# A hybrid encoder layer on one core: the diagonal's mask moves from GpSimd into the logits' PSUM bank

## The chip, the cores and the metric

The kernel runs on one core of a Trainium2 chip. The core has a matrix engine (TensorE, PE in the profile; its weight loads are PEld), a vector engine (VectorE, DVE), an activation engine (ScalarE, ACT), a general engine (GpSimd, POOL) and SyncE (SP), which only issues DMAs. The engines run at the same time. Each takes its own instructions strictly in order and waits on semaphores. TensorE writes to PSUM, which has eight banks of 128 x 512 float32; GpSimd works on SBUF alone in this kernel, VectorE and ScalarE on both.

The metric is the device time of one execution in microseconds; less is better.

## The reference

One layer on 2048 tokens of width 1024: a norm, a projection, three mixers side by side (two short convolutions and a stick-breaking attention), an output projection, then a squared-ReLU MLP of width 4096 and a last norm. The change touches the attention, and one step of the norms. The attention, for each block of 128 queries:

```python
z = jnp.einsum("bhqd,bhkd->bhqk", qb, kb).astype(jnp.float32) * scale   # scale = 1/8
mask = s_idx < t_idx
log_beta = jax.nn.log_sigmoid(z)
log_1m = jnp.where(mask, log_beta - z, 0.0)
suffix = lax.cumsum(log_1m, axis=3, reverse=True) - log_1m
a = jnp.where(mask, jnp.exp(log_beta + suffix), 0.0)
out = jnp.einsum("bhqk,bhkd->bhqd", a, vb)
```

In products instead of logarithms: a = sigmoid(z) times the product of sigmoid(-z) over all later allowed keys. A key that the mask forbids must give sigmoid(z) = 0 and sigmoid(-z) = 1.

## The kernel before

All matrix products are split in two float32r halves, high and low, so that most products are three matmuls (`mm3`), and many tensors are split (`split`, lines 85 to 90): ScalarE copies the high half, VectorE or GpSimd subtracts it.

The work has two stages. The first makes the projections, the convolutions and, woven between them, the attention of the first 512 queries (i = 0) for the eight heads. The second runs four blocks of 512 tokens (`block`, line 818): output projection, then 32 units of the first MLP product (`ffn1`, tile ps_u) and eight groups of the second (`ffn2`, tile ps_y, added into `acc` by VectorE in line 944). Between the matmuls of the first three blocks lies the attention for i = 1, 2, 3: 24 groups (head, i) of 512 queries. `weave` (line 57) lets the attention advance in step with the main work. This gives the order in which the program is written; a planner then orders each engine's instructions by a model of their times, and each engine keeps that order on the chip.

A group goes through these steps:

- `a_load` (line 489): GpSimd issues the two DMAs of tile KQd, the group's own keys and queries. There is one buffer; it comes free after the last logits of the group before.
- `a_pass1` (line 539), first part: three diagonal steps n = 0, 1, 2, each on two blocks of 128 x 256. `a_z` (line 509) makes the logits z by matmuls into a bank with tag z (three banks in the second stage). `a_diag` (line 524) takes two sigmoids by ScalarE (`om` of -z, line 529, `t` of z, line 530) into SBUF and masks both by GpSimd's affine_select (line 534; fill 1 and 0). Then products: the left half of `om` into the right half of `t` (GpSimd, lines 558 and 566), and the halves of `om` into the running products `Rd` and `R` (VectorE, lines 559, 568, 573, 575); GpSimd multiplies the third `t` by `R` (line 574).
- `a_cross_a` (line 603): VectorE transposes `Rd` into `T` in 32 x 32 blocks, a scan (line 611) makes the products along the keys into tile `O`, small products (line 619) join the four parts, and line 625 writes the result back to `T`.
- for i > 0, 4i steps with all 128 x 512 logits of earlier keys (lines 585 to 600): ScalarE puts sigmoid(z) in SBUF and sigmoid(-z) back in z's own bank, GpSimd multiplies (line 595), VectorE goes on with the product `R` from the bank (line 597). Then `a_cross_a` again.
- `a_pass2` (line 629): VectorE transposes the result into PSUM (ps_q) and multiplies each `t` by it (lines 646, 653), the product is split by ScalarE and GpSimd (lines 88, 90, tiles Ahi, Alo), and TensorE multiplies it by the values into ps_o.

In `block`, after the first two units of `ffn1`, the mean square is spread over a bank with tag z (`spread`, line 130); ScalarE copies it to SBUF as `ms` (line 963), and VectorE multiplies the eight tiles `acc` by it (line 965).

`A0`, `om`, `R`, `O` and so on are tiles of pools with a fixed number of buffers; `self.ab` (line 1050 for the second stage) holds these numbers. The function `finish_` makes the last norm of a block; it too uses banks with tag z.

Of the kernel before, what the change touches and what calls it, by code (L numbers as in the profile page):

```python
# [7 lines left out]
F32 = mybir.dt.float32  # L8
F32R = mybir.dt.float32r
I32 = mybir.dt.int32  # L10
AF = mybir.ActivationFunctionType
ALU = mybir.AluOpType
# [3 lines left out]
P = 128  # L16
# [3 lines left out]
TB = 512  # L20
# [5 lines left out]
HP = 200  # L26
PRE = 4
LEFT = (0, 0, 0, 1, 0, 0, 0, 1)
RMS_EPS = 1e-6
LN_EPS = 1e-5  # L30

# [37 lines left out]
class Trunk:  # L69
# [126 lines left out]
    def attention_consts(self, ctx):  # L196
        nc = self.nc
        c = ctx.enter_context(self.tc.tile_pool(name="aconsts", bufs=1))
        self.d1 = c.tile([P, 16, 33], F32, name="d1")
        nc.vector.memset(self.d1, 0.0)  # L200
        nc.vector.memset(self.d1[:, :, 32:33], 1.0)


    def p_pools(self, ctx):
# [57 lines left out]
    def norm_sum(self, g):  # L262
        self.rv[g] = self.rsqrt(self.colsum([self.ss[g]], "o" if g else "q"), 1.0 / D, RMS_EPS)

# [256 lines left out]
        k = keys.rearrange("c (a p b) -> c a p b", a=2, b=J // 2)  # L521
        return [k[:, j % 2, :, j // 2] for j in range(J)]

    def a_diag(self, z, n):

        nc, pool, ab = self.nc, self.at, self.ab
        t = pool.tile([P, TB], F32, name="A0", tag="A0", bufs=ab["A0"])
        om = pool.tile([P, TB], F32, name="om", tag="om", bufs=ab["om"])
        nc.scalar.activation(om, z, AF.Sigmoid, scale=-0.125)
        nc.scalar.activation(t, z, AF.Sigmoid, scale=0.125)  # L530
        base, cm = ((-1, -2), (256 - 3, -4), (256 - 1, -4))[n]
        for x, fill in ((om, 1.0), (t, 0.0)):
            x = x.rearrange("p (h c) -> p h c", h=2)
            nc.gpsimd.affine_select(
                out=x, in_=x, pattern=[[1, 2], [1, 256]], compare_op=ALU.is_gt, fill=fill, base=base, channel_multiplier=cm
            )
        return t, om

    def a_pass1(self, g):
        nc, pool, i = self.nc, self.at, g["i"]  # L540
        ab = self.ab
        lo, hi2 = slice(0, 256), slice(256, 512)

        def new(name, bufs, shape=(P, TB), dt=F32):
            return pool.tile(list(shape), dt, name=name, tag=name, bufs=bufs)

        if i:
            g["Kl"] = pool.tile([P, self.kmax], F32R, name="Kl", tag="Kl", bufs=self.ab["Kl"])
            for rows, kq in self.kq_halves(g["h"]):
                to = g["Kl"][rows, : TB * i].rearrange("c (j q) -> c j q", j=2)  # L550
                self.load_r(to, kq[:, 0, :, : TB * i // 2])
        A0 = g["A0"] = []
        Rd = new("Rd", 1)

        k2 = [g["Kd"][:, 0:P], g["Kd"][:, 256 : 256 + P]]
        z = self.a_z(g, [(k2[1], lo, lo), (k2[0], lo, hi2)])
        t, om = self.a_diag(z, 0)
        nc.gpsimd.tensor_tensor(t[:, hi2], t[:, hi2], om[:, lo], op=ALU.mult)
        nc.vector.tensor_tensor(Rd[:, lo], om[:, lo], om[:, hi2], op=ALU.mult)
        A0.append(t)  # L560
        yield 1

        k4 = self.every(g["Kd"], 4)
        z = self.a_z(g, [(k4[3], hi2, lo), (k4[2], hi2, hi2)])
        t, om = self.a_diag(z, 1)
        nc.gpsimd.tensor_tensor(t[:, hi2], t[:, hi2], om[:, lo], op=ALU.mult)
        R = new("R", ab["R"])
        nc.vector.tensor_tensor(R[:, lo], om[:, lo], om[:, hi2], op=ALU.mult)
        A0.append(t)
        yield 1  # L570
        z = self.a_z(g, [(k4[1], hi2, lo), (k4[0], hi2, hi2)])
        t, om = self.a_diag(z, 2)
        nc.vector.tensor_tensor(R[:, hi2], om[:, lo], R[:, lo], op=ALU.mult)
        nc.gpsimd.tensor_tensor(t, t, R, op=ALU.mult)
        nc.vector.tensor_tensor(Rd[:, hi2], om[:, hi2], R[:, hi2], op=ALU.mult)
        A0.append(t)
        yield 1
        tot = self.a_cross_a(g, Rd, None)
        if not i:
            return  # L580
        J = 4 * i
        kl = self.every(g["Kl"][:, : TB * i], J)
        full = slice(0, TB)
        R = None
        for j in range(J - 1, -1, -1):
            z = self.a_z(g, [(kl[j], full, full)])
            t = new("A0", ab["A0"])
            if R is None:
                nc.scalar.activation(t, z, AF.Sigmoid, scale=0.125)
                R = new("R", 2)  # L590
                nc.scalar.activation(R, z, AF.Sigmoid, scale=-0.125)
            else:
                nc.scalar.activation(t, z, AF.Sigmoid, scale=0.125)  # L593
                nc.scalar.activation(z, z, AF.Sigmoid, scale=-0.125)  # L594
                nc.gpsimd.tensor_tensor(t, t, R, op=ALU.mult)  # L595
                Rn = new("R", 2)
                nc.vector.tensor_tensor(Rn, z, R, op=ALU.mult)  # L597
                R = Rn
            A0.append(t)
            yield 1  # L600
        self.a_cross_a(g, R, tot)

    def a_cross_a(self, g, R, seed):

        nc, pool = self.nc, self.at
        T = pool.tile([P, 16, 33], F32, name="T", tag="T1" if seed is None else "T2", bufs=1)
        nc.gpsimd.memset(T[:, :, 32:33], 0.0)
        nc.vector.transpose(T[:, :, 0:32], R)
        O = pool.tile([P, 16, 33], F32, name="O", tag="O", bufs=1)
        fl = lambda x: x.rearrange("p a b -> p (a b)")[:, ::-1]  # L610
        nc.vector.tensor_tensor_scan(fl(O), fl(T), fl(self.d1), 1.0, op0=ALU.mult, op1=ALU.add)
        C = self.tiny.tile([P, 16], F32, name="C", tag="C", bufs=3)
        if seed is None:
            nc.gpsimd.memset(C[96:128], 1.0)
        else:
            nc.vector.tensor_copy(C[96:128], seed)
        for a in (2, 1, 0):
            s, d = slice(32 * a + 32, 32 * a + 64), slice(32 * a, 32 * a + 32)
            nc.vector.tensor_tensor(C[d], C[s], O[s, :, 0], op=ALU.mult)
        tot = None  # L620
        if seed is None:
            tot = self.tiny.tile([32, 16], F32, name="tot", tag="tot", bufs=2)
            nc.vector.tensor_tensor(tot, C[0:32], O[0:32, :, 0], op=ALU.mult)
        qt = T[:, :, 0:32]
        nc.vector.tensor_tensor(qt, O[:, :, 1:33], C.unsqueeze(2).to_broadcast([P, 16, 32]), op=ALU.mult)
        g["qd" if seed is None else "ql"] = qt
        return tot

# [189 lines left out]
    def block(self, tb, before):  # L818
# [3 lines left out]
        nc, a, hp = self.nc, self.a, self.hp  # L822
# [34 lines left out]
        ss = hp.tile([P, TB], F32, name="ss", tag="ss", bufs=2)  # L857
# [35 lines left out]
        fh, fl = {}, {}  # L893
# [64 lines left out]
        mt = self.small("mt")  # L958
        nc.vector.tensor_scalar(mt, self.colsum([ss], "z"), 1.0 / D, RMS_EPS, op0=ALU.mult, op1=ALU.add)
        em = self.small("em")  # L960
        nc.vector.scalar_tensor_tensor(em, mt, RMS_EPS, mt, op0=ALU.mult, op1=ALU.mult)
        ms = hp.tile([P, TB], F32, name="ms", tag="ss", bufs=2)
        nc.scalar.activation(ms, self.spread(mt, "z"), AF.Copy)
        for d in range(DC):
            nc.vector.tensor_tensor(acc[d], acc[d], ms, op=ALU.mult)
        ss2 = hp.tile([P, TB], F32, name="ss2", tag="ss", bufs=2)
# [14 lines left out]
        else:  # L981
# [4 lines left out]
            with self.tc.high_priority(offset=HP):  # L986
                for n, _ in enumerate(ffn2(FC // G - 1, right, again=1)):
                    for _ in range(LEFT[n]):
                        next(fin, None)
# [25 lines left out]
    def build(self):  # L1015
        tc = self.tc
        with ExitStack() as ctx:
# [24 lines left out]
            with ExitStack() as c2:  # L1042
                self.psum_pool(c2, d=3, z=3, q=1, o=1)
                self.at = c2.enter_context(tc.tile_pool(name="at2", bufs=1, reuse_waits="tile"))
                self.st = c2.enter_context(tc.tile_pool(name="st2", bufs=1, reuse_waits="tile"))
                self.ha = c2.enter_context(tc.tile_pool(name="ha", bufs=1, reuse_waits="tile"))
                self.hp = c2.enter_context(tc.tile_pool(name="hp", bufs=1, reuse_waits="tile"))
                self.ob = 2
                self.kmax = 1536
                self.ab = dict(KQd=1, Kl=1, A0=15, om=2, R=2, Alo=3, Ahi=3, Vl=2, late=2, yc=1)  # L1050
                at = Side(self.attention([(h, i) for i in (1, 2, 3) for h in range(H)]))
                self.heads = {}

                def attend(i):
                    while self.heads.get(i, 0) < H:
                        at.advance(at.done + 1)

                self.attend = attend
                self.end = iter(())
                for tb in range(4):  # L1060
                    weave(self.block(tb, self.end), [(at, (74, 95, 107)[tb], 45, 365 if tb < 2 else 320, False)] if tb < 3 else [])
# [48 lines left out]
```

## Time and profile before

| | |
|---|---|
| median of 3 runs | 2451.35 us |
| lowest and highest | 2446.44 and 2455.63 us |
| the profiled execution | 2458.28 us |
| its span in the trace | 2456.6 us |
| mean granted TensorE clock | 0.99 |

The profile is of one execution. Busy time of an engine is the time in which it has an instruction of its own in work. A row of groups reads: line, engine, operation, tiles written and read, shapes, count; then busy microseconds in all, the mean in nanoseconds of one, and the idle time of the engine just before these instructions with what ended it. A row of waits reads: the instruction that waited, what released it, microseconds in all, how many times, the longest. A row of the timeline reads: start and duration in microseconds, engine, line, operation. The granted clock is the share of full speed that TensorE was given. DMA rows tell the time from issue to landing.

### The profile page before, as it was taken

The numbers are of one execution on the slowest core, as the hardware profiler recorded it, in microseconds if no ns is written. First come the engines' busy times: TensorE is split into PE (matmuls) and PEld (weight loads), VectorE is DVE, ScalarE is ACT, GpSimd is POOL, SyncE is SP. The second block draws the span as 40 slices with busy tenths as digits, with TensorE's granted clock in tenths as the row PEclk, the third lists the DMA queues.
The fourth block names the chain that finished last, engine by engine and source line by source line (L and its number), as shares of the span: only waits on it lengthen the run. The fifth ranks groups of instructions, "written<-read, shape, count | busy, mean of one in ns | idle before, by whom it ended". The sixth has DMA issues, their size and how long they took to land.

```text
span 2456.6 us, 32414 instructions
## 1 busy us (share of the span) xinstructions
PE 2395.6 (98%) x11316; PEld 2017.3 (82%) x11316; DVE 1627.6 (66%) x2348; ACT 1033.6 (42%) x1910; POOL 1163.9 (47%) x1221
## 2 busy tenths in 40 slices
PE   8999998999999999999999999999999999999998
PEld 7889876898778878787878888888888888888887
DVE  7957799943988878767977768677666735212114
ACT  5232522333566556534545555345555532121121
POOL 1342576641667666515666677158888830000000
PEclk9999999999999999999999999999999999999999
DMA  7579977888688878687778777776666656655555
GB/s 262 189 257 333 298 247 208 239 280 265 161 244 226 230 196 211 175 287 234 218 211 250 241 231 212 243 240 190 183 204 194 199 178 204 242 195 186 200 187 189
DMA packets 236036, 549.05 MB, mean 224 GB/s; under 512 B 25696, under 2 KB 99424, under 8 KB 217440
## 3 DMA queue, kind: packets, MB, share of 16 engines
q1 hardware_dynamic: 162896, 464.11, 54.8%
q0 software_dynamic: 53888, 73.42, 15.8%
q10 hardware_dynamic: 19088, 9.44, 1.3%
q8 instruction: 90, 1.47, 0.2%
q14 instruction: 74, 0.61, 0.1%
HBM read 390.38 MB, written 148.11 MB: 219 GB/s over the span
## 4 chain that ended last, share of the span: by engine, by line
PE 81%; DVE 9%; DMA 6%; issue 2%; ACT 1%; POOL 1%; POOLq 0%; SPq 0%; DVEq 0%; ACTq 0%
PE ps_y L103 8%; PE ps_y L107 8%; PE ps_y L105 8%; PE ps_u L103 8%; PE ps_u L105 8%; PE ps_u L107 8%; PE ps_p L107 4%; PE ps_p L105 4%; PE ps_p L103 4%; DMA KQd<-KQ 2%; PE ps_z L515 2%; PE ps_x L103 2%; PE ps_x L105 2%; PE ps_x L107 2%; PE ps_z L516 2%; DMA w<-s_w 2%
## 5 line engine op out<-in xcount | busy, mean ns | idle before, releaser
L90 POOL TENSOR_TENSOR Alo<-A,Ahi 128x512 fp32r<-128x512 f32 x288 | 394.3, 1380 | 105.7 <-PE ps_o L700 45.9
L944 DVE TENSOR_TENSOR acc<-acc,ps_y 128x512 f32<-128x512 f32 (+1 forms) x264 | 174.8, 666 | 178.0 <-PE ps_y L107 176.6
L103 PE MATMUL ps_y<-fh,w 128*128 128x512 f32 (+1 forms) x1056 | 282.9, 386 | 6.9 <-DVE acc L944 4.5
L103 PE MATMUL ps_u<-hh,w 128*128 128x512 f32 x1024 | 280.2, 394 | 7.7 <-DMA w<-s_w 4.8
L107 PE MATMUL ps_y<-fl,w 128*128 128x512 f32 (+1 forms) x1056 | 279.6, 385 | 1.0 <-DVE fl L919 1.0
L105 PE MATMUL ps_y<-fh,w 128*128 128x512 f32 (+1 forms) x1056 | 279.6, 385 | 0.0
L105 PE MATMUL ps_u<-hh,w 128*128 128x512 f32 x1024 | 278.0, 393 | 0.0
L595 POOL TENSOR_TENSOR A<-A,R 128x512 f32<-128x512 f32 x168 | 232.5, 1385 | 93.7 <-ACT A L593 69.6
L107 PE MATMUL ps_u<-hl,w 128*128 128x512 f32 x1024 | 276.6, 391 | 0.0
L909 ACT ACTIVATE ps_u<-ps_u 128x512 f32<-128x512 f32 x128 | 74.7, 584 | 460.0 <-PE ps_u L107 460.0
L118 POOL TENSOR_TENSOR rs_y<-rs_v,mhalf 128x4 f32<-128x4 f32 (+1 forms) x13 | 14.9, 1149 | 522.0 <-DVE rs_v L117 485.1
L103 PEld LDWEIGHTS ps_y<-fh,w 128*128 128x128 f32 x1056 | 193.2, 188 | 46.7 <-DVE acc L944 4.9
L103 PEld LDWEIGHTS ps_u<-hh,w 128*128 128x128 f32 x1024 | 191.5, 190 | 47.2 <-DMA w<-s_w 6.1
L107 PEld LDWEIGHTS ps_y<-fl,w 128*128 128x128 f32 x1056 | 195.6, 189 | 40.6 <-DVE fl L919 1.6
L105 PEld LDWEIGHTS ps_u<-hh,w 128*128 128x128 f32 x1024 | 194.3, 190 | 41.4 <-DVE w L90 0.2
L105 PEld LDWEIGHTS ps_y<-fh,w 128*128 128x128 f32 x1056 | 195.4, 188 | 39.7
L107 PEld LDWEIGHTS ps_u<-hl,w 128*128 128x128 f32 x1024 | 193.1, 189 | 40.2
L88 ACT ACTIVATE Ahi<-A 128x512 fp32r<-128x512 f32 x288 | 177.5, 628 | 92.9 <-PE ps_o L699 37.0
L919 DVE TENSOR_TENSOR fl<-ps_u,fh 128x512 fp32r<-128x512 f32 x128 | 87.5, 685 | 194.6 <-ACT fh L918 194.2
L597 DVE TENSOR_TENSOR R<-ps_z,R 128x512 f32<-128x512 f32 x168 | 115.4, 687 | 147.8 <-ACT ps_z L594 108.9
L452 DVE SCALAR_TENSOR_TENSOR ps_c<-g,wb,ps_c 128x512 f32<-128x512 f32 x240 | 179.8, 749 | 4.8
L88 ACT ACTIVATE w<-wraw 128x512 fp32r<-128x512 f32 x152 | 92.1, 628 | 182.4 <-PE ps_y L107 115.8
(173 smaller groups left out, 4952.2 us busy)
## 6 DMA issues: line engine op xcount, KB each, us to landing
w<-s_w SPq DMA_DIRECT2D x200, 512.0 KB, 3.5
w<-s_w SPq DMA_DIRECT2D x68, 1024.0 KB, 4.8
wraw<-in_w SPq DMA_DIRECT2D x192, 256.0 KB, 4.9
w<-s_w_out SPq DMA_DIRECT2D x64, 512.0 KB, 4.8
s_w<-w SPq DMA_DIRECT2D x32, 1024.0 KB, 5.5
s_w<-w SPq DMA_DIRECT2D x56, 512.0 KB, 5.2
KQd<-KQ POOLq DMA_DIRECT2D x64, 384.0 KB, 7.1
xraw<-in_xT SPq DMA_DIRECT2D x48, 256.0 KB, 4.8
```

Of the source, the lines that this page charges most:

```text
L88: nc.scalar.activation(hi, x, AF.Copy)
L90: e.tensor_tensor(lo, x, f(hi), op=ALU.subtract)
L103: self.nc.tensor.matmul(ps, wh, xh, start=start and k == 0, stop=False)
L105: self.nc.tensor.matmul(ps, wl, xh, start=False, stop=False)
L107: self.nc.tensor.matmul(ps, wh, xl, start=False, stop=stop and k == n - 1)
L452: nc.vector.scalar_tensor_tensor(t, g[:, k : k + TB], self.wb[:, c, k : k + 1], t, op0=ALU.mult, op1=ALU.add)
L515: nc.tensor.matmul(z[:, oc], keys, g["qh"][:, qc], start=k == 0, stop=False)
L595: nc.gpsimd.tensor_tensor(t, t, R, op=ALU.mult)
L597: nc.vector.tensor_tensor(Rn, z, R, op=ALU.mult)
L909: nc.scalar.activation(ps, ps, AF.Relu)
L919: nc.vector.tensor_tensor(lo, ps, f(hi), op=ALU.subtract)
L944: nc.vector.tensor_tensor(acc[d][:, cols], acc[d][:, cols], ps, op=ALU.add)
```

## The change

Three edits.

1. For i > 0, the mask of the diagonal steps is a number added to the logits. Two constant tiles `far` (128 x 260) hold 0 where a key is allowed and -1e30 where it is not; a window of 257 columns, read with an offset of one column for the second half, serves the two blocks of a step. VectorE adds it to z in place in the PSUM bank. ScalarE then takes sigmoid(z) into `t`, and sigmoid(-z) back into the bank: in step n = 2 all of it, in steps 0 and 1 the left half, while the right half goes to a new SBUF tile `oh` of 256 columns with two buffers. GpSimd's selects are left out, and VectorE in place of GpSimd multiplies the right half of `t` by the left half of sigmoid(-z) in steps 0 and 1. For i = 0 the diagonal is as before.
2. The scan of `a_cross_a` writes over its input `T`; tile `O` is gone, and the results lie one column further.
3. `ms` stays in the bank in which `spread` made it, without ScalarE's copy; VectorE reads it there.

In the second stage `om` has one buffer in place of two; it serves only `otmp` there.

```diff
+        self.far = []
+        for n, (base, cm) in enumerate(((-1, -2), (253, -4))):
+            t = c.tile([P, 260], F32, name=f"far{n}")
+            nc.gpsimd.memset(t, 0.0)
+            nc.gpsimd.affine_select(out=t, in_=t, pattern=[[1, 260]], compare_op=ALU.is_gt, fill=FAR, base=base, channel_multiplier=cm)
+            self.far.append(t)
...
-    def a_diag(self, z, n):
+    def a_diag(self, z, n, far):
 
         nc, pool, ab = self.nc, self.at, self.ab
         t = pool.tile([P, TB], F32, name="A0", tag="A0", bufs=ab["A0"])
+        if far:
+
+            m = self.far[n > 0][:, 2 * (n > 1) : 2 * (n > 1) + 257]
+            m = bass.AP(m.tensor, m.offset, [m.ap[0], [1, 2], [1, 256]])
+            x = z.rearrange("p (h c) -> p h c", h=2)
+            nc.vector.tensor_tensor(x, x, m, op=ALU.add)
+            nc.scalar.activation(t, z, AF.Sigmoid, scale=0.125)
+            if n == 2:
+                nc.scalar.activation(z, z, AF.Sigmoid, scale=-0.125)
+                return t, z[:, 0:256], z[:, 256:512]
+            oh = pool.tile([P, 256], F32, name="oh", tag="oh", bufs=2)
+            nc.scalar.activation(z[:, 0:256], z[:, 0:256], AF.Sigmoid, scale=-0.125)
+            nc.scalar.activation(oh, z[:, 256:512], AF.Sigmoid, scale=-0.125)
+            return t, z[:, 0:256], oh
...
-        t, om = self.a_diag(z, 0)
-        nc.gpsimd.tensor_tensor(t[:, hi2], t[:, hi2], om[:, lo], op=ALU.mult)
-        nc.vector.tensor_tensor(Rd[:, lo], om[:, lo], om[:, hi2], op=ALU.mult)
+        t, om, om2 = self.a_diag(z, 0, i > 0)
+
+        (nc.vector if i else nc.gpsimd).tensor_tensor(t[:, hi2], t[:, hi2], om, op=ALU.mult)
+        nc.vector.tensor_tensor(Rd[:, lo], om, om2, op=ALU.mult)
...
-        O = pool.tile([P, 16, 33], F32, name="O", tag="O", bufs=1)
         fl = lambda x: x.rearrange("p a b -> p (a b)")[:, ::-1]
-        nc.vector.tensor_tensor_scan(fl(O), fl(T), fl(self.d1), 1.0, op0=ALU.mult, op1=ALU.add)
+        nc.vector.tensor_tensor_scan(fl(T), fl(T), fl(self.d1), 1.0, op0=ALU.mult, op1=ALU.add)
...
-        qt = T[:, :, 0:32]
-        nc.vector.tensor_tensor(qt, O[:, :, 1:33], C.unsqueeze(2).to_broadcast([P, 16, 32]), op=ALU.mult)
+        qt = T[:, :, 1:33]
+        nc.vector.tensor_tensor(qt, qt, C.unsqueeze(2).to_broadcast([P, 16, 32]), op=ALU.mult)
...
-        ms = hp.tile([P, TB], F32, name="ms", tag="ss", bufs=2)
-        nc.scalar.activation(ms, self.spread(mt, "z"), AF.Copy)
+        ms = self.spread(mt, "z")
...
-                self.ab = dict(KQd=1, Kl=1, A0=15, om=2, R=2, Alo=3, Ahi=3, Vl=2, late=2, yc=1)
+                self.ab = dict(KQd=1, Kl=1, A0=15, om=1, R=2, Alo=3, Ahi=3, Vl=2, late=2, yc=1)
```

Steps n = 1 and n = 2 take their products in the same way: `om` and `om2` are what `a_diag` returns, and in step 1 the product into `t` goes to VectorE for i > 0.

More of the change, by code (lines that the diff above doesn't have):

```diff
@@ L28 @@
 LEFT = (0, 0, 0, 1, 0, 0, 0, 1)
+FAR = -1e30
 RMS_EPS = 1e-6
@@ L536, in a_diag @@
             )
-        return t, om
+        return t, om[:, 0:256], om[:, 256:512]
     def a_pass1(self, g):
@@ L564, in a_pass1 @@
         z = self.a_z(g, [(k4[3], hi2, lo), (k4[2], hi2, hi2)])
-        t, om = self.a_diag(z, 1)
-        nc.gpsimd.tensor_tensor(t[:, hi2], t[:, hi2], om[:, lo], op=ALU.mult)
+        t, om, om2 = self.a_diag(z, 1, i > 0)
+        (nc.vector if i else nc.gpsimd).tensor_tensor(t[:, hi2], t[:, hi2], om, op=ALU.mult)
         R = new("R", ab["R"])
-        nc.vector.tensor_tensor(R[:, lo], om[:, lo], om[:, hi2], op=ALU.mult)
+        nc.vector.tensor_tensor(R[:, lo], om, om2, op=ALU.mult)
         A0.append(t)
@@ L571, in a_pass1 @@
         z = self.a_z(g, [(k4[1], hi2, lo), (k4[0], hi2, hi2)])
-        t, om = self.a_diag(z, 2)
-        nc.vector.tensor_tensor(R[:, hi2], om[:, lo], R[:, lo], op=ALU.mult)
+        t, om, om2 = self.a_diag(z, 2, i > 0)
+        nc.vector.tensor_tensor(R[:, hi2], om, R[:, lo], op=ALU.mult)
         nc.gpsimd.tensor_tensor(t, t, R, op=ALU.mult)
-        nc.vector.tensor_tensor(Rd[:, hi2], om[:, hi2], R[:, hi2], op=ALU.mult)
+        nc.vector.tensor_tensor(Rd[:, hi2], om2, R[:, hi2], op=ALU.mult)
         A0.append(t)
@@ L618, in a_cross_a @@
             s, d = slice(32 * a + 32, 32 * a + 64), slice(32 * a, 32 * a + 32)
-            nc.vector.tensor_tensor(C[d], C[s], O[s, :, 0], op=ALU.mult)
+            nc.vector.tensor_tensor(C[d], C[s], T[s, :, 0], op=ALU.mult)
         tot = None
@@ L622, in a_cross_a @@
             tot = self.tiny.tile([32, 16], F32, name="tot", tag="tot", bufs=2)
-            nc.vector.tensor_tensor(tot, C[0:32], O[0:32, :, 0], op=ALU.mult)
-        qt = T[:, :, 0:32]
-        nc.vector.tensor_tensor(qt, O[:, :, 1:33], C.unsqueeze(2).to_broadcast([P, 16, 32]), op=ALU.mult)
+            nc.vector.tensor_tensor(tot, C[0:32], T[0:32, :, 0], op=ALU.mult)
+        qt = T[:, :, 1:33]
+        nc.vector.tensor_tensor(qt, qt, C.unsqueeze(2).to_broadcast([P, 16, 32]), op=ALU.mult)
         g["qd" if seed is None else "ql"] = qt
```

## The prediction

> **What bounds the kernel now.** The head of the page comes first: which engine is busy all the time, and how far the others are from it.
>
> ```profile
> span 2456.6 us, 32414 instructions
> PE 2395.6 (98%) x11316; PEld 2017.3 (82%) x11316; DVE 1627.6 (66%) x2348; ACT 1033.6 (42%) x1910; POOL 1163.9 (47%) x1221
> ```
>
> TensorE is the bound: 98%. The change takes no matmul away, so it can only shorten time in which TensorE stands still or runs at a lower clock. The second view is therefore the table of windows, cut where attention with earlier keys (i = 1, 2, 3) begins and ends. Its columns are the stretch, its length, then PE, PEld, DVE, ACT and POOL busy, the granted clock, and DMA.
>
> ```profile
> 0.00:605.00 605.00, 584.18 (x3036) 498.87 (x3037) 451.16 (x656) 207.71 (x382) 269.37 (x284) 0.99 0.79 257
> 605.00:1300.00 695.00, 666.35 (x3024) 555.74 (x3023) 557.44 (x765) 374.62 (x700) 407.49 (x452) 0.98 0.78 221
> 1300.00:2000.00 700.00, 698.35 (x3178) 588.45 (x3177) 492.67 (x720) 362.71 (x674) 484.62 (x483) 1.00 0.70 212
> 2000.00:2456.00 456.00, 446.70 (x2083) 374.20 (x2081) 126.32 (x208) 88.62 (x155) 2.43 (x3) 0.99 0.58 201
> ```
>
> The mask is rebuilt only for i > 0, so only the two middle stretches hold new instructions. TensorE idles there for 695.0 - 666.35 + 700.0 - 698.35 = 30.3 us. The clock of 0.98 costs about another 0.02 x 695 = 13.9 us. **So 44 us, 1.8%, is all that the changed part can win.** VectorE is busy 1050.1 of 1395 us and GpSimd 892.1: neither is full, but VectorE has 80% between 605 and 1300.
>
> The third view says what TensorE waits for between 605 and 2000; its rows give the sum, the number of times and the longest.
>
> ```profile
> PE ps_z L515 <- DMA KQd<-KQ: 15.2, 6, 5.5
> PE ps_y L103 <- DVE acc L944: 4.5, 4, 2.6
> PE ps_u L103 <- DMA w<-s_w: 3.6, 3, 2.1
> PE ps_u L103 <- DVE acc L944: 2.3, 1, 2.3
> PE ps_y L103 <- DVE fl L919: 2.2, 2, 1.6
> PE ps_y L107 <- DVE fl L919: 1.0, 2, 0.7
> PE ps_o L700 <- POOL Alo L90: 0.9, 1, 0.9
> PE ps_u L103 <- ACT A L530: 0.6, 1, 0.6
> ```
>
> They add up to the 30.3 us. DMA holds 18.8 (15.2 + 3.6); the other engines being late holds 11.5, of which VectorE's `acc` is 6.8, `fl` 3.2, and GpSimd and ScalarE 1.5. Most of it lies before 1300: the stretch after it has 1.65 us of idle time in all.
>
> **What is removed.** For 24 (head, i) groups the masking on GpSimd and the products that read `om` from SBUF go. From the groups by line between 600 and 2000:
>
> ```profile
> L534 POOL TENSOR_SCALAR_AFFINE_SELECT om<-om 128x512 f32<-128x512 f32 x72 | 51.3, 713 | 51.9 <-ACT om L529 51.5
> L534 POOL TENSOR_SCALAR_AFFINE_SELECT A<-A 128x512 f32<-128x512 f32 x72 | 50.5, 701 | 0.0
> L566 POOL TENSOR_TENSOR A<-A,om 128x256 f32<-128x256 f32 x24 | 19.9, 828 | 0.5
> L558 POOL TENSOR_TENSOR A<-A,om 128x256 f32<-128x256 f32 x24 | 18.3, 761 | 0.9
> L568 DVE TENSOR_TENSOR R<-om 128x256 f32<-128x256 f32 x24 | 26.0, 1083 | 6.1 <-POOL om L534 6.1
> L965 DVE TENSOR_TENSOR acc<-acc,ms 128x512 f32<-128x512 f32 x24 | 23.3, 1039 | 3.2 <-ACT ms L963 3.2
> L559 DVE TENSOR_TENSOR Rd<-om 128x256 f32<-128x256 f32 x24 | 21.5, 894 | 6.7 <-POOL om L534 6.7
> L573 DVE TENSOR_TENSOR R<-om,R 128x256 f32<-128x256 f32 x24 | 17.6, 732 | 11.7 <-POOL om L534 11.7
> L575 DVE TENSOR_TENSOR Rd<-om,R 128x256 f32<-128x256 f32 x24 | 15.0, 625 | 0.7
> ```
>
> GpSimd loses 51.3 + 50.5 + 19.9 + 18.3 = 140.0 us, of 892.1. VectorE loses 26.0 + 21.5 + 17.6 + 15.0 = 80.1 for the `om` products and 23.3 for `acc` times `ms`, 103.4 together.
>
> **What is added**, priced by rows of like shape with one operand in PSUM; 256-column and ps_c rows are of the whole run.
>
> ```profile
> L944 DVE TENSOR_TENSOR acc<-acc,ps_y 128x512 f32<-128x512 f32 x180 | 121.5, 679 | 61.1 <-PE ps_y L107 60.3
> L944 DVE TENSOR_TENSOR acc<-acc,ps_y 128x256 f32<-128x256 f32 x16 | 6.7, 421 | 4.3 <-PE ps_y L107 3.7
> L452 DVE SCALAR_TENSOR_TENSOR ps_c<-g,wb,ps_c 128x512 f32<-128x512 f32 x240 | 179.8, 749 | 4.8
> L804 DVE TENSOR_TENSOR ss<-ss,sq 128x512 f32<-128x512 f32 x29 | 19.9, 685 | 3.8 <-ACT sq L803 3.7
> L803 ACT ACTIVATE sq<-acc 128x256 f32<-128x256 f32 x13 | 5.4, 418 | 14.8 <-DVE acc L944 13.6 <-DVE rs_v L117 1.1
> L529 ACT ACTIVATE om<-ps_z 128x512 f32<-128x512 f32 x72 | 42.9, 596 | 58.9 <-DVE Rd L559 34.2 <-PE ps_z L516 24.5
> L963 ACT ACTIVATE ms<-ps_R 128x512 f32<-128x512 f32 x3 | 1.8, 586 | 0.0
> ```
>
> VectorE gets 72 mask adds. No row here adds two tensors into PSUM: 679 ns (into SBUF) and 749 ns (into PSUM, with a per-partition scalar) bound it; I take 690, nearer to the same operation. 72 x 0.690 = 49.7 us (48.9 to 53.9). The six products of a group, two of them come from GpSimd, now read `om` or its half in PSUM: 144 x 0.421 = 60.6. The 24 products with `ms` in PSUM: 24 x 0.679 = 16.3. Together 126.6 against 103.4 removed: **VectorE gets 23 us more over 1395**, about 1 us a group, inside its 345 us of idle time.
>
> Why is a 256-column product at 894 to 1083 ns to become 421? The removed rows read two SBUF operands, and such instructions stretch while GpSimd runs products. The plainest place:
>
> ```profile
> 978.96 7.68 DVE L611 TENSOR_TENSOR_SCAN O<-T,d 128x528 f32<-128x528 f32 x1
> 978.54 1.74 POOL L90 TENSOR_TENSOR Alo<-A,Ahi 128x512 fp32r<-128x512 f32 x1
> 979.81 1.73 POOL L595 TENSOR_TENSOR A<-A,R 128x512 f32<-128x512 f32 x1
> 981.06 1.72 POOL L90 TENSOR_TENSOR Alo<-A,Ahi 128x512 fp32r<-128x512 f32 x1
> 983.49 2.03 POOL L90 TENSOR_TENSOR Alo<-A,Ahi 128x512 fp32r<-128x512 f32 x1
> ```
>
> A scan of two SBUF tensors ended only after GpSimd's row of splits did. The 679 ns of L944 against 1039 of L965 say the same: equal shape, one operand in PSUM or none. The scan in its own place still reads two SBUF tensors and keeps this stretch; I cost that edit at 0, since the buffer `O` never ended a wait in these rows and VectorE works in order anyway.
>
> [...]
>
> ScalarE: two of a group's three sigmoids of -z are cut in halves: 4 x 0.418 - 2 x 0.596 = 0.48 us, 24 x 0.48 = 11.5, less 1.8 for the `ms` copies. It is busy 737 of 1395, so nothing by itself. The two far masks add four GpSimd operations of 260 columns at the start. The nearest row:
>
> ```profile
> 1.08 0.29 POOL masks.py:199 TENSOR_SCALAR_AFFINE_SELECT ident<-ident 128x128 f32<-128x128 f32 x1
> ```
>
> At up to the 713 ns of a 512-column select they are under 3 us, on an engine that the windows show busy for 269 of the first 605 us; cost 0, and at worst those 3 us.
>
> **Waits that go.** VectorE waited 6.1 + 11.7 + 6.7 = 24.5 us for GpSimd's selects (rows above). ScalarE waited 34.2 us in L529 for `Rd` L559 to free one of two `om` buffers; behind it in ScalarE's queue stand the activations that make `fh`, so this is where `fl` and L530 come late. The half `oh` has two buffers for two uses a group, so that wait should vanish. I let the 3.2 (`fl`), 0.9 and 0.6 us of TensorE's waits go, and a quarter of the 6.8 of `acc`, since scans and the small products of L619 keep their stretch: 4.7 + 1.7 = 6.4 us. With 13.9/30.3 = 0.46 us of lost clock for each idle microsecond it would be 9.3; the gaps concerned are short, so I take **8 us**.
>
> **Waits that come.** The mask add stands in VectorE's queue and waits for the logits' matmul; behind it are `acc` and `fl`, for which TensorE waits. Bounds: 0 to the 24.5 us that VectorE waited at the same place before. And a logits bank is held longer: formerly until L530, now until VectorE has read the half that stays in it. The nearest rows are TensorE's waits above: blocks of full keys hold their bank until VectorE's L597, 168 times, and no row has ps_z or anything else wait for L597. Against that stands 0.6 us for L530. Between 0 and 24 x 0.8 us I take **2 us**, near to the row. `ms` holds one of three banks through eight products, 8 x 0.679 = 5.4 us a block in place of 0.6, at the start of a block where one attention group begins; cost 0 to 3 x 1.5 us, taken as 0 because TensorE has other matmuls there.
>
> **The transfer that stays.** The largest wait, 15.2 us, is the load of a group's own keys and queries.
>
> ```profile
> DMA to landing us min/median/max: 4.4/7.3/16.8
> L83 POOL DMA_DIRECT2D KQd<-KQ x46 | 31.9, 714 | 46.9 <-PE ps_z L516 33.4 <-PE ps_o L699 8.8 <-PE ps_o L700 3.6
> ```
>
> GpSimd issues it, and a less loaded GpSimd might issue earlier. But the issue itself already waits 33.4 us for L516, the last logits that read the old tile: the end of those matmuls, not GpSimd's work, mostly sets the issue. What stalls TensorE is a landing near 16.8 us rather than 7.3. I cost this at 0.
>
> **Sum.** -8 + 2 = -6 us against the profiled execution's 2458.28 us (its span 2456.6 and 1.7 around it): 2452. That execution lies 6.9 us above the median of 2451.35, so by the median: **2445 us**, with 2437 to 2451 for this case alone.
>
> **Rivals.**
>
> Slower: the bank ring. A group issues its three diagonal logits close together, which fills all three banks; the next group of full keys needs one, and it now comes free only after a VectorE add, ScalarE's three sigmoids and two products, behind whatever VectorE is stuck on (7.68 us in the row above). At 0.8 us a group: 24 x 0.8 x 1.46 = 28 us, less the 6, gives 2473. It decides from (6 + 12.3)/(24 x 1.46) = 0.52 us a group. For it: VectorE at 80% before 1300. Against it: no wait for L597.
>
> Faster: the key loads profit too. If half of their stalls goes with its clock (15.2 x 1.46/2 = 11.1) and all 11.5 us of late engines: 2429. For it: the clock's 13.9 us follow the idle time. Against it: the 33.4 us above.
>
> No effect: each engine's order of instructions is made anew by the planner, so the stalls merely move, and 140 us taken from GpSimd are worth nothing because it was never the bound: 2451.
>
> **Chances.** The forecast 0.44, slower 0.16, faster 0.26, no effect 0.14. A measurement of this kernel can tell about 0.5%, 12.3 us: under 2439 lie the faster rival and 0.09 of the forecast's, 0.35; above 2463.6 lies 0.15; between them 0.50. The range from 2426 to 2466 leaves out the far half of both outer rivals.
>
> **What would show it.** Right, if the selects of L534 are gone for i > 0, GpSimd's busy time falls by some 140 us, VectorE's rises by 5 to 40, its 256-column products lie near 421 ns, the 34.2 us of ScalarE's wait are gone, and TensorE's waits for `fl` and `acc` fall from 10.0 us to about 5 while those for KQd stay near 15. Wrong, if TensorE waits for ps_z on VectorE in many groups (slower), or if KQd's waits fall below 8 us (faster).

## The result, and the profile after

| | before | after |
|---|---|---|
| median of 22 runs each | 2450.22 us | 2454.89 us |
| lowest and highest | 2446.44 and 2460.41 us | 2447.24 and 2460.87 us |
| ratio, 95% interval | 1 | 1.0021 (1.0011 to 1.0030) |

The change costs about 5 us, 0.2%. That is inside the predicted range and inside half a percent, but on the other side of what was forecast: 6 us less. The profiled execution of the changed kernel took 2449.74 us, below its own median, that of the kernel before 2458.28 us, above its own. The two spans compared directly would give the opposite sign; only parts of the traces that repeat from one execution to the next may be compared.

The head of the page and the windows of the changed kernel, cut as before (columns: stretch, length, PE, PEld, DVE, ACT, POOL, clock, DMA share, GB/s):

```profile
span 2447.7 us, 32293 instructions
PE 2391.7 (98%) x11316; PEld 2013.6 (82%) x11316; DVE 1606.3 (66%) x2468; ACT 1041.0 (43%) x1954; POOL 1025.6 (42%) x1033
```

```profile
605.00:1300.00 695.00, 676.14 (x3099) 565.63 (x3098) 546.58 (x857) 388.27 (x744) 338.57 (x354) 0.99 0.77 224
1300.00:2000.00 700.00, 690.00 (x3124) 579.11 (x3123) 487.57 (x750) 354.72 (x672) 413.04 (x388) 1.00 0.69 210
```

GpSimd's load fell as worked out: 1163.9 - 1025.6 = 138 us less. VectorE's did not rise by 23 us but fell by 21, over the whole span. TensorE's idle time between 605 and 2000 stayed in these two traces: 18.9 + 10.0 = 28.9 us, against 30.3. But it moved: after 1300 it was 1.65 us and is 10.0. In a second trace of each kernel it is 3.5 and 11.8 us there, so this part repeats.

TensorE's waits of the changed kernel in the same stretch:

```profile
PE ps_z L523 <- DMA KQd<-KQ: 7.5, 3, 3.5
PE ps_y L104 <- DVE acc L967: 5.2, 3, 2.6
PE ps_u L104 <- DMA w<-s_w: 4.7, 6, 1.3
PE ps_z L523 <- DVE R L621: 3.2, 2, 2.1
PE ps_y L108 <- DVE fl L942: 2.9, 1, 2.9
PE ps_z L523 <- ACT R L615: 1.7, 1, 1.7
PE ps_o L723 <- POOL Alo L91: 1.3, 2, 0.8
PE ps_y L104 <- ACT w L98: 1.3, 1, 1.3
PE ps_x L104 <- DMA w<-s_w_out: 0.4, 1, 0.4
PE ps_o L714 <- DVE yc L697: 0.4, 1, 0.4
PE ps_z L523 <- ACT ps_u L932: 0.2, 1, 0.2
```

Split by what ended them: DMAs 12.6 us (18.8 before), other engines 16.2 us (11.5 before). Among the rows that an engine ended, three are new for ps_z: the logits now wait 5.1 us (3.2 + 1.7 + 0.2) for banks that VectorE's L621 and ScalarE have not read yet.

What holds these up stands in the groups by line (busy us, mean ns, then the idle time before and what ended it):

```profile
L541 DVE TENSOR_TENSOR ps_z<-ps_z,far 128x512 f32<-128x512 f32 x72 | 47.5, 691 | 0.7 <-PE ps_z L524 0.6
L542 ACT ACTIVATE A<-ps_z 128x512 f32<-128x512 f32 x72 | 42.9, 596 | 66.2 <-DVE ps_z L541 66.2
L581 DVE TENSOR_TENSOR A<-A,ps_z 128x256 f32<-128x256 f32 x24 | 10.0, 417 | 16.8 <-ACT oh L548 16.8
L592 DVE TENSOR_TENSOR R<-ps_z,oh 128x256 f32<-128x256 f32 x24 | 10.0, 417 | 0.0
L987 DVE TENSOR_TENSOR acc<-acc,ps_R 128x512 f32<-128x512 f32 x24 | 14.6, 682 | 7.2 <-PE ps_R L135 7.2
```

VectorE idled 0.7 us in all ahead of its 72 adds: the logits were nearly always there before VectorE came to the add. ScalarE idled 66.2 us for the same adds. Ahead of the diagonal's first sigmoid it had idled 58.9 us before the change (34.2 for `Rd`, 24.5 for the logits), so the change did not free ScalarE there; it gave it another wait. The add stands in VectorE's queue behind other work, and ScalarE's queue stands behind the add. One place in the timeline, from the last logits of a step to the stall:

```profile
1674.86 0.28 PE L524 MATMUL ps_z<-KQd 128*128 128x256 f32 x1
1677.86 5.45 DVE L676 TENSOR_TENSOR A<-A,ps_q 128x512 f32<-128x512 f32 x9
1683.24 0.69 DVE L541 TENSOR_TENSOR ps_z<-ps_z,far 128x512 f32<-128x512 f32 x1
1683.96 0.60 ACT L542 ACTIVATE A<-ps_z 128x512 f32<-128x512 f32 x1 [3.10 <-DVE ps_z L541]
1684.97 0.59 ACT L613 ACTIVATE A<-ps_z 128x512 f32<-128x512 f32 x1
1685.45 0.59 ACT L615 ACTIVATE R<-ps_z 128x512 f32<-128x512 f32 x1
1686.10 0.62 PE L523 MATMUL ps_z<-KQd,Kl 128*128 128x512 f32 x1 [1.73 <-ACT R L615]
```

The logits end at 1675.1. Nine products of an earlier group occupy VectorE from 1677.86, so the add comes 8.1 us later. ScalarE has nothing it may do for 3.10 us. The two sigmoids of the next logits, which TensorE had finished by 1679.4, come behind it, and only then is their bank free: TensorE stands for 1.73 us.

### The profile page after: what moved, and what is told of

Read it like the earlier page. It is cut to its first block, busy times and chain, and to the rows that moved or that the text cites. A ratio compares the mean times of both kernels' runs of the same rounds, so it can differ in the third digit from the quotient of the medians.

```text
span 2447.7 us, 32293 instructions
## 1 busy us (share of the span) xinstructions
PE 2391.7 (98%) x11316; PEld 2013.6 (82%) x11316; DVE 1606.3 (66%) x2468; ACT 1041.0 (43%) x1954; POOL 1025.6 (42%) x1033
## 4 chain that ended last, share of the span: by engine, by line
PE 79%; DVE 10%; DMA 6%; issue 2%; ACT 1%; POOL 1%; POOLq 0%; SPq 0%; DVEq 0%; ACTq 0%
PE ps_y L104 8%; PE ps_y L108 8%; PE ps_y L106 8%; PE ps_u L106 7%; PE ps_u L104 7%; PE ps_u L108 7%; PE ps_p L104 4%; PE ps_p L108 4%; PE ps_p L106 4%; DMA w<-s_w 3%; PE ps_z L523 2%; PE ps_x L104 2%; PE ps_x L106 2%; PE ps_x L108 2%; PE ps_z L524 2%
## 5 line engine op out<-in xcount | busy, mean ns | idle before, releaser
L619 POOL TENSOR_TENSOR A<-A,R 128x512 f32<-128x512 f32 x168 | 225.8, 1347 | 126.2 <-ACT A L617 99.5
L621 DVE TENSOR_TENSOR R<-ps_z,R 128x512 f32<-128x512 f32 x168 | 115.6, 688 | 141.0 <-ACT ps_z L618 99.6
L91 DVE TENSOR_TENSOR w<-wraw,w 128x512 fp32r<-128x512 f32 x152 | 145.6, 976 | 29.9 <-ACT w L89 29.5
```

The lines of the kernel that those rows point to most:

```text
L91: e.tensor_tensor(lo, x, f(hi), op=ALU.subtract)
```

## The experiments

Four ideas were to be told apart. **A**: the place of the add, VectorE's queue ahead of ScalarE's. **B**: banks held until VectorE's products. **C**: the third edit, `ms`, with C2: VectorE's added work. **D**: any edit makes the planner order the engines anew, and that alone moves the time. Each time below is of 9 to 12 runs (6 with three om buffers; the first measurement of the changed kernel has 22), and its ratio is to runs of the kernel before beside it. "Late engines" is the sum of TensorE's waits between 605 and 2000 us that no DMA ended, added up from that view of each run.

| run | ratio (95%) | late engines, us | ended by DMAs, us |
|---|---|---|---|
| before, first trace | | 11.5 | 18.8 |
| before again | 0.9995 (0.9974 to 1.0016) | 12.8 | 13.1 |
| ms only | 1.0004 (0.9987 to 1.0022) | 11.9 | 15.2 |
| scan only | 0.9992 (0.9978 to 1.0006) | 12.9 | 16.6 |
| scan and ms | 1.0005 (0.9988 to 1.0022) | 11.1 | 14.6 |
| changed kernel, first trace | 1.0021 (1.0011 to 1.0030) | 16.2 | 12.6 |
| changed kernel again | 1.0007 (0.9994 to 1.0021) | 17.5 | 15.8 |
| add at higher priority | 1.0006 (0.9988 to 1.0023) | 16.1 | 18.7 |
| mask and scan | 1.0021 (1.0008 to 1.0035) | 17.5 | 12.9 |
| add, om in SBUF | 1.0005 (0.9987 to 1.0023) | 16.4 | 11.8 |
| no add | 0.9968 (0.9952 to 0.9984) | 9.6 | 15.1 |
| add behind ScalarE | 0.9985 (0.9964 to 1.0005) | 11.4 | 16.7 |
| mask behind ScalarE | 0.9995 (0.9978 to 1.0013) | 11.5 | 18.2 |
| three om buffers | 1.0081 (1.0055 to 1.0107) | 23.3 | 21.9 |

**Which edit.** The kernel before with one edit alone:

```diff
-        ms = hp.tile([P, TB], F32, name="ms", tag="ss", bufs=2)
-        nc.scalar.activation(ms, self.spread(mt, "z"), AF.Copy)
+        ms = self.spread(mt, "z")
```

> The kernel before, with only the third edit: ms stays in its bank. Theory A (the loss of 0.21% comes from the mask's edit) expects 0 to -0.1% against before, with the products of acc by ms near 680 ns instead of 950. Theory C (the loss comes from ms holding one of three banks at a block's start) expects +0.1 to +0.2%, with waits of TensorE for a z bank near the blocks' starts.

```diff
-        nc.vector.tensor_tensor_scan(fl(O), fl(T), fl(self.d1), 1.0, op0=ALU.mult, op1=ALU.add)
+        nc.vector.tensor_tensor_scan(fl(T), fl(T), fl(self.d1), 1.0, op0=ALU.mult, op1=ALU.add)
```

> The kernel before, with only the second edit: the scan writes over T. Theories A and C expect 0 within 0.1%, since the scan still reads two SBUF tensors. A rival D (every edit makes the planner order the engines' work anew, and the order alone moves the time by some 5 us either way) expects a change of 0.1 to 0.2% here too, though nothing of weight was edited.

And the changed kernel with ScalarE's copy of `ms` put back:

> The changed kernel without its third edit: ScalarE copies ms to SBUF again. (The mask's edit alone does not fit in SBUF.) Theory A expects the whole loss to stay, +0.15 to +0.3% against before. Theory C expects it gone, 0 or below.

Neither small edit moves the time by what these runs can tell, and late engines stay at 11.9 and 12.9 us. The time of `ms` alone, 1.0004, would still allow C's +0.1 to +0.2%, but no wait for a logits' bank that an engine ended is in that trace, where C expected it. With the mask's edit and ScalarE's copy back, late engines are 17.5 and the ratio lies above 1; C expected the loss gone. That takes C out. D does not hold as a general rule: two new orders came without a cost that these runs can tell. The loss is in the mask's edit.

**How far one trace holds.** The changed kernel and the kernel before, each once more:

> The changed kernel once more, for a second trace and as a measure beside the others: +0.2% against before by all theories. Theory A expects in the trace, between 605 and 2000 us, ScalarE's wait for the mask's add at 55 to 75 us again, and TensorE's waits that no DMA ended at 14 to 19 us again (11.5 in the kernel before); if these move by more than 5 us from one execution to the next, they can't carry the argument.

> The kernel before, unchanged, for a second trace and for how far apart two measurements of one kernel lie: a ratio of 1 within 0.1%, and TensorE's waits that no DMA ended at 11 to 13 us.

TensorE's waits of the kernel before in its second trace:

```profile
PE ps_z L515 <- DMA KQd<-KQ: 6.9, 4, 4.0
PE ps_u L103 <- DMA w<-s_w: 5.7, 4, 2.8
PE ps_y L103 <- DVE acc L944: 4.6, 4, 2.6
PE ps_y L103 <- DVE fl L919: 3.8, 2, 2.2
PE ps_u L103 <- DVE acc L944: 2.3, 1, 2.3
```

The wait for KQd was 15.2 us in the first execution and is 6.9 here, with nothing changed; VectorE's 4.5 and 2.3 come back as 4.6 and 2.3. The sum of waits that an engine ended repeats within about 1.5 us, that of waits that a DMA ended moves by up to 6. The changed kernel's second measurement, 1.0007, is lower than its first and its interval reaches 1; the loss is thus known only as some 2 to 5 us, and only the first measurement is clear of 1 by itself. Its late engines came back at 17.5, and ScalarE's wait for the add at 64.6.

**The add itself.** The changed kernel without it:

```diff
-            nc.vector.tensor_tensor(x, x, m, op=ALU.add)
```

> The changed kernel with the add of the mask left out (nothing masks the diagonal then, for i > 0); sigmoid(-z) still stays in its bank. Theory A (ScalarE's queue waits for the add in VectorE's queue) expects ScalarE's wait of 65 to 78 us at L542 gone, TensorE's waits that no DMA ended down from 16 to 17.5 us to 11 to 13, and -0.15 to -0.3% against the changed kernel, so 0 to -0.1% against before. Rival B (the banks are held until VectorE's products) expects these waits to stay at 16 or more and +0.1 to +0.2% against before.

ScalarE then waited 13.3 us ahead of these sigmoids, 12.9 of it for the logits:

```profile
L541 ACT ACTIVATE A<-ps_z 128x512 f32<-128x512 f32 x72 | 41.5, 593 | 13.3 <-PE ps_z L524 12.9 <-issue 0.2
```

Late engines fell to 9.6 us and the time to 0.9968: 8 us under the kernel before, the clearest gain of the study, and more than A expected (0 to -0.1%). Late engines are only 2 to 3 us under those of the kernel before; where the other 5 us come from is not shown. B is not needed: the banks are held until VectorE's products here too. But the run takes away two things at once, the wait and 47.5 us of VectorE's work. So the same work was put behind the sigmoids, with a tile of zeros:

```diff
-FAR = -1e30
+FAR = 0.0
...
-            nc.vector.tensor_tensor(x, x, m, op=ALU.add)
...
                 nc.scalar.activation(z, z, AF.Sigmoid, scale=-0.125)
+                nc.vector.tensor_tensor(x, x, m, op=ALU.add)
                 return t, z[:, 0:256], z[:, 256:512]
...
             nc.scalar.activation(oh, z[:, 256:512], AF.Sigmoid, scale=-0.125)
+            nc.vector.tensor_tensor(x, x, m, op=ALU.add)
             return t, z[:, 0:256], oh
```

> As the run without the add, but VectorE adds a tile of zeros in the same place and shape behind ScalarE's sigmoids (nothing masks the diagonal for i > 0): VectorE's work is that of the changed kernel, and ScalarE no longer waits for it. Theory A (the place: ScalarE's queue behind VectorE's) expects TensorE's waits that no DMA ended at 9 to 12 us and -0.15 to -0.35% against before, like the run without the add. Rival C2 (the 50 us of VectorE's work in the adds) expects 15 to 18 us and +0.05 to +0.2%.

ScalarE now waits for the logits, not for the add:

```profile
L541 ACT ACTIVATE A<-ps_z 128x512 f32<-128x512 f32 x72 | 41.5, 593 | 14.2 <-PE ps_z L524 14.1
```

Late engines: 11.4 us, as A expects, not the 15 to 18 of C2. The time, 0.9985, lies at the edge of what A named (-0.15%), and its interval just reaches 1. Against the changed kernel it is clear of the first measurement (1.0011 to 1.0030), not of the other two. Some of TensorE's waits of that run:

```profile
PE ps_y L104 <- DVE acc L968: 4.8, 4, 2.6
PE ps_x L104 <- DMA w<-s_w_out: 3.1, 2, 2.8
PE ps_z L523 <- DVE R L622: 2.2, 2, 1.2
PE ps_y L104 <- DVE fl L943: 2.2, 2, 1.7
```

The same work in another place, and the waits for logits' banks are 2.2 us in place of 5.1 (0.3 more follow an issue); the waits for GpSimd's `Alo` (1.3 and 2.2 us in the two traces of the changed kernel) and for `yc` (0.4) are gone. The difference of 9.6 and 11.4 us, and of 0.9968 and 0.9985, may be the work's own price; the intervals overlap.

**The banks.** The add as in the changed kernel, but sigmoid(-z) goes to `om` in SBUF with two buffers, and GpSimd multiplies:

```diff
             nc.scalar.activation(t, z, AF.Sigmoid, scale=0.125)
-            if n == 2:
-                nc.scalar.activation(z, z, AF.Sigmoid, scale=-0.125)
-                return t, z[:, 0:256], z[:, 256:512]
...
+            om = pool.tile([P, TB], F32, name="om", tag="om", bufs=ab["om"])
+            nc.scalar.activation(om, z, AF.Sigmoid, scale=-0.125)
+            return t, om[:, 0:256], om[:, 256:512]
```

> The mask's add as in the changed kernel, but sigmoid(-z) goes to om in SBUF (two buffers) as before, so a bank comes free when ScalarE has read it, and GpSimd makes the two products as before. Rival B expects TensorE's waits that no DMA ended at 11 to 13 us and 0 against before. Theory A expects 16 us or more, with the waits for z banks of 4.9 us still there, and +0.1 to +0.3% against before.

ScalarE's wait and TensorE's two longest that an engine ended, from the two views of waits of this run:

```profile
ACT A L542 <- DVE ps_z L541: 80.9, 26, 6.9
```

```profile
PE ps_y L104 <- DVE acc L963: 5.5, 5, 2.6
PE ps_z L523 <- DVE R L617: 5.3, 4, 2.5
```

The diagonal's banks come free early now, yet the waits for logits' banks are still there (5.3, and 1.0 in two smaller rows), and late engines stay at 16.4 us. The time, 1.0005, can't tell A from B; the waits can, and they speak for A.

**Two tries to mend it.** The add at a higher priority in the planner's order:

```diff
-            nc.vector.tensor_tensor(x, x, m, op=ALU.add)
+            with self.tc.high_priority(offset=HP):
+                nc.vector.tensor_tensor(x, x, m, op=ALU.add)
```

> The changed kernel with the add at a higher priority in the planner's order, so that it stands ahead of products that were ready earlier in VectorE's queue. Theory A expects ScalarE's wait for the add at under 45 us, TensorE's waits that no DMA ended at 11 to 14 us, and -0.05 to -0.2% against the changed kernel. Rival B expects no change against it.

The planner put every instruction of every engine in the same order as without it, as the traces show, so this is a third measurement of the changed kernel (1.0006, late engines 16.1), and the idea of an earlier add was not tried. The other puts the masking behind ScalarE:

```diff
-            nc.vector.tensor_tensor(x, x, m, op=ALU.add)
...
                 nc.scalar.activation(z, z, AF.Sigmoid, scale=-0.125)
+                nc.vector.tensor_tensor(x, x, m, op=ALU.max)
+                select(t, 0.0, 0)
                 return t, z[:, 0:256], z[:, 256:512]
...
+            select(oh, 1.0, 1)
+            select(t, 0.0, 0)
+            nc.vector.tensor_tensor(x[:, 0], x[:, 0], m[:, 0], op=ALU.max)
```

> The diagonal masked behind ScalarE, with the right result: VectorE takes the larger of sigmoid(-z) in its bank and a tile of ones at forbidden places, GpSimd selects t and the half in SBUF. ScalarE never waits for VectorE. Theory A expects ScalarE's wait of 65 us gone and -0.1 to -0.35% against before. If VectorE's or GpSimd's work is what counts, 0 to +0.2%.

Here `select` is GpSimd's affine_select of before, the far tiles hold 1 at forbidden places, and in steps 0 and 1 ScalarE makes `oh` first. Late engines are back at 11.5 us. The time, 0.9995, lies between what A named (-0.1% or less) and what its rival named (0 or more) and decides nothing: by the waits this mends the change, by the time it can't be told from the kernel before, nor clearly from the changed one. Here, too, logits wait for a bank that one of the diagonal's products still reads:

```profile
PE ps_z L523 <- DVE Rd L595: 1.5, 1, 1.5
PE ps_z L523 <- DVE R L605: 0.5, 1, 0.5
```

That is B's mechanism at 2.0 us, so it is not nothing, but it is not the loss.

**Was ScalarE's old wait a cost?** The prediction took it for one. The kernel before with the second and third edits, with three buffers for `om` and with two:

```diff
-                self.ab = dict(KQd=1, Kl=1, A0=15, om=2, R=2, Alo=3, Ahi=3, Vl=2, late=2, yc=1)
+                self.ab = dict(KQd=1, Kl=1, A0=15, om=3, R=2, Alo=3, Ahi=3, Vl=2, late=2, yc=1)
```

> The kernel before with the second and third edits and a third buffer for om, which takes the place of the tile O; the mask stays on GpSimd. ScalarE's wait of 34.2 us for Rd L559 should be gone. If that wait made TensorE wait, as the prediction assumed, TensorE's waits that no DMA ended fall from 11.5 to 8 us or less and the time by 0.1 to 0.2%; if not, both stay within 2 us and 0.1%.

> The kernel before with the second and third edits and two om buffers: the run with three om buffers but for the buffer. If the third buffer made that run slow, this lies within 0.1% of before with TensorE's waits that no DMA ended at 11 to 13 us; if the two edits together did, it lies 0.5% or more above.

ScalarE's longest wait ahead of `om`, and TensorE's longest waits, with three buffers:

```profile
ACT om L529 <- PE ps_z L516: 14.2, 11, 5.4
```

```profile
PE ps_z L515 <- DMA KQd<-KQ: 15.6, 6, 4.6
PE ps_z L515 <- DVE R L597: 5.9, 5, 2.0
PE ps_y L103 <- DVE fl L918: 5.9, 2, 5.6
PE ps_y L103 <- DVE acc L943: 5.8, 4, 2.6
```

ScalarE's wait for `Rd` is gone from that run's list, and the kernel is 0.8% slower, with late engines at 23.3 us. With two buffers it is at 1.0005 and 11.1. So the third buffer did it, and taking that wait away in this way is no gain; it was not taken away alone. By what way the buffer makes `fl` and the banks late was not followed further; the planner's order changes with it, so D may hold here, and this stays open.

## Why the prediction was wrong, point by point

- **The bound** was right: TensorE is busy 98% before and after. The 44 us for the middle part were those of one execution: the second trace of the kernel before has 26.0 us of idle time there in place of 30.3, and a clock of 0.99 in place of 0.98 between 605 and 1300. The 0.46 us of lost clock for each idle microsecond rested on that 0.98 alone.
- **GpSimd's 140 us** came (138), and no gain in time came with them, as the rival "no effect" had it.
- **VectorE's 23 us more** did not come; between 605 and 2000 it is busy 16 us less (1050.1 to 1034.2). The single prices were good: the add 691 ns (690 taken), the 256-column products 417 (421), `acc` times `ms` 682 (679). What was left out is what VectorE does beside: in two traces before and two after, the small products of `C` fell from 71.6 and 71.4 us to 58.8 and 59.2, the copies of `tot` from 10.3 and 9.3 to 4.1 and 6.0, the splits of w from 152.7 and 150.8 to 144.2 and 147.0. That GpSimd's lighter load did this is not shown: with mask and scan, where GpSimd is as light (756 us in this stretch, 752 in the changed kernel), the splits of w took 154.1 us.
- **Waits that go: the step that failed.** The prediction let ScalarE's 34.2 us wait for an `om` buffer vanish and with it 4.7 us of TensorE's waits, because `oh` has buffers enough. The wait for `om` did vanish; a wait of 66.2 us for the add came in the same queue. TensorE's waits for `fl` went from 3.2 and 4.8 us in the two traces before to 2.9 and 3.5, and those for `Alo` did not go (0.9 before, 1.3 after). Those for `acc` went from 6.8 and 6.9 to 5.2 and 5.2, the quarter that was named, but by luck: they are 4.8 us with the third edit alone, 4.8 with scan and `ms`, and 7.1 both with the scan alone and with mask and scan. So they fell with `ms` in its bank, not with the waits that the prediction let go. And with three buffers the old wait went without any gain.
- **Waits that come** were looked for on the wrong engine. The working asked who stands behind the add in VectorE's queue, and how long VectorE would wait for the logits; that was 0.7 us. The price was paid by who stands behind the add in ScalarE's queue: 5.1 us of waits for logits' banks where 2 were allowed, and with them some waits for `Alo` (1.3) and `yc` (0.4), which are gone when the add stands behind ScalarE. The 1.3 us for ScalarE's `w` are not of this making, since they stay without the add. The evidence cited against it, that no row waits for L597, held in the traces of the kernel before; in the changed kernel the same line, L621 there, has 3.2 us.
- **The sum**: late engines were to fall by 6.4 and rise by 2; they rose from 11.5 and 12.8 to 16.2, 17.5 and 16.1, some 4.4 us by the means, near to the 2 to 5 us of the time. No lost clock shows beside it: the mean granted clock of the runs is 0.993 for both kernels.
- **The key loads** were costed at 0, but expected to stay near 15 us. That number was one execution's: 6.9 us in the second. The changed kernel's 7.5 us lie under the 8 that were to speak for the faster rival; with 6.9 in the unchanged kernel they say nothing for it.
- **The rivals**: the slower one named the bank ring and VectorE's queue, with 0.52 us a group as its point. The banks' waits came to 5.1/24 = 0.2 us a group: its mechanism in part, under its point, and through ScalarE.

## What to carry to other kernels

When an operation moves from one engine to another, ask not only what stands behind it in its new queue, but which third engine's queue now stands behind it, and how late the new engine usually is: VectorE, busy 70 to 80% here, was late for the add (66.2 us of ScalarE's waiting), and handed its lateness on to everything in order behind the consumer. A wait that an engine shows need not cost the bound engine anything (ScalarE's 34.2 us for `Rd` went with a third buffer, and the kernel got no faster), and one that does may be named in none of its rows, as here the add; so remove a wait in an experiment before counting on it. And take two traces before building on a wait that a DMA ended: the one for KQd was 15.2 us, then 6.9.

## What the runs showed of the hardware

On VectorE, products of two SBUF tensors took very unequal times in the kernel before: `Rd` from the halves of `om` (L559, 256 columns) 397 to 4107 ns, 894 in the mean, and `acc` times `ms` (L965, 512 columns) 681 ns in the middle but up to 2205. Between 605 and 2000 us, the four of L559 with no GpSimd instruction beside them took 410 to 417 ns, the 15 that overlapped a GpSimd product 1132 in the mean; of L965, ten took 678 to 694 without GpSimd, ten 1539 in the mean with its products. In the changed kernel, with one operand in PSUM, the same products took 402 to 419 ns (L582) and 680 to 689 (L987), and 417 and 682 in the mean where they overlapped a GpSimd product (3 and 15 of 24). The long ones fit the prediction's reading that GpSimd's products stretch them; no run isolates it. An add from and into PSUM cost 691 ns (L541), near one between SBUF tiles (685, L804 before). ScalarE's 256-column sigmoid took 377 ns into PSUM (L547) and 395 into SBUF (L548). The shorter products did not shorten the kernel: with all of them it stands at 1.0021, with those of `acc` and `ms` alone at 1.0004.
